# Chain products of an RWKV-7 layer issued in turn for the two column halves, and their output copy issued a step later

## The chip, the cores and the metric

The kernel runs on one core of a Trainium2 chip. The metric is the device time of one execution in microseconds, from the runs of the kernel before: 2830.11 us median of three (2828.12 to 2833.1). Times inside an execution come from one profiled execution.

## The reference

One layer takes x (2048 frames of 1024 channels), projects it, and feeds two token mixers: an S5 state space on 512 channels and an RWKV-7 recurrence of eight heads of width 64. Their outputs go through an output projection, a norm and a residual, then through a squared-ReLU feed-forward network. The part that the change touches is the recurrence:

```python
def step(S, inp):
    r_t, w_t, k_t, v_t, kk_t, a_t = inp
    sa = jnp.einsum('bhvk,bhk->bhv', S, -kk_t)
    S = (S * w_t[:, :, None, :]
         + sa[..., None] * (kk_t * a_t)[:, :, None, :]
         + v_t[..., None] * k_t[:, :, None, :])
    return S, jnp.einsum('bhvk,bhk->bhv', S, r_t)
```

The kernel computes it in chunks of 64 frames: inside a chunk with matrices (Gram products and a triangular inverse), from chunk to chunk with the state.

## The kernel before

The work has two stages. Stage one (`phase1`) handles four blocks of 512 frames; each block has four units of two heads, so 16 units. A unit is projected by dense 128x128 by 512 products (`preps`), gets Gram products and inverses, and then its chain of eight chunks runs (`chain`, line 1212). The 16 chains run one after another, 128 steps in all. The S5 mixer and part of the output projection run beside them. Stage two (`phase2`) has the gates, the output projection, the norms and the feed-forward products, which use a Strassen-Winograd scheme with sums of tiles on VectorE.

The order of all instructions is made by a planner in the kernel's own Python. Every kind of work is a generator; `merge` (line 447) always advances the one with the earliest due time by the planner's own clock, shifted by a constant for its kind (`OFFSETS`, line 249). `BURST` and `MARGIN` (line 247) pull forward the dense kinds (`DENSE`) of stage one when the planner thinks that TensorE has too little work in a stretch of time. `B1` and `B2` (line 245) weigh elementwise steps that read PSUM, for stage one and two. The planner prices a product in `price` (line 144); its flag `nc.pair` lowers the price of a single-precision product from 1.68 to 0.88 ns a column. It changes no instruction. The Gram products (line 1062) already set it. Every engine executes its instructions in the order in which they are emitted.

One step of a chain (loop from line 1222) works on one PSUM tile `cu` of two:
- two products of `wr` with `sv` into `uo` (partitions 0 to 63 and 64 to 127), and on GpSimd the decayed state `s0p`
- a copy of the upper half of `uo` to `rs`, on VectorE or ScalarE, whichever the planner has free
- two products of the inverse with `rs` into `us`, and a copy of it, negated, into `sv`
- two state products of `bet` with `sv` into `ss`: 128 rows, 64 columns, output in partitions 0 to 63
- two output products of `lat` (`lb` in the code) with `sv` into `uo[64:128]`: 64 rows, 64 columns, output in partitions 64 to 127
- the state sum `ss + s0p` on VectorE, the input of the next step, and on ScalarE the copy of `uo[64:128]` to the unit's output tile `ot`, and the signal `("ch", unit, step)`

Each of these products is single precision and appears in the trace as two records. The group norm (`gnorm`, line 1263) and the reuse of Gram buffers wait for the signals. Since one helper issues every instruction, all rows of the trace name line 108; tiles tell the work apart.

Of the kernel before, what the change touches and what calls it, by code (L numbers as in the profile page):

```python
# [241 lines left out]


D, NL, SR, TR, GR = 4, 2, 6, 14, 3
B1, B2 = 467, 4782
ORDER, ORDER0 = 'ugkrv', 'krugv'
SLACK, BURST, MARGIN = 199, 3048, 300
DENSE = ('preps', 'rwouts')
OFFSETS = {'s5_tables': -42, 's5_params': -395, 'norms': 352, 'inputs': -39, 'finals': 122, 'rwouts': -625, 'substitutes': -68, 'dense': -786, 'posts': -223, 'hns': 688, 's5_lane': 1208, 'chains': -22, 'zfirst': 262, 'inverses': 214, 's5_setup': 208, 'toks': 77, 'gramss': -173, 'x_loads': -2522, 'rwin': -59, 'f_loads': -91}


KEPT = ("w_in", "heads")
# [2 lines left out]
class K:  # L255
# [191 lines left out]
    def merge(self, streams):  # L447
# [6 lines left out]
        while any(x not in self.kept for x in h) or self.eq:  # L454
            r = [x for x in h if x[3] is None]
            b = BURST if nc.needy(MARGIN) else 0.0
            x = min(r, key=lambda x: (x[1] - (b if x[0].__name__ in DENSE else 0.0)
                                      + OFFSETS.get(x[0].__name__, 0.0), x[2])) if r else None
            e = self.elem()
# [752 lines left out]
    def chain(self, u):  # L1212
        nc, ep = self.nc, self.ep
        yield from self.need(("inv", u["s"]), ("bet", u["s"], 1), ("sv", u["s"]), "s5p")
        b, j, pc, wr, lb, bet, sv, yb = (u[n] for n in ("b", "j", "pc", "wr", "lb", "bet", "sv", "yb"))
        st = self.st[j // 2][64 * (j % 2):64 * (j % 2) + 64]
        nc.scalar.copy(sv[0][0:64, :, 0, :], st)
        if u["s"] >= 2:
            yield from self.need(("gno", u["s"] - 2))
        ot = u["ot"] = self.t(ep, [128, 4, 2, 64], "ot", bufs=2)  # L1220
        yield
        for c in range(8):
            q, i = divmod(c, 4)
            cu = self.t(self.pcu, [128, 384], "cu")
            uo = cu[:, 0:128].rearrange("p (h v) -> p h v", h=2)
            us = cu[0:64, 128:256].rearrange("p (h v) -> p h v", h=2)
            ss = cu[0:64, 256:384].rearrange("p (h v) -> p h v", h=2)
            for h in range(2):
                nc.tensor.matmul(uo[:, h, :], lhsT=wr[q][:, h, i, :], rhs=sv[q][:, h, i, :], start=h == 0, stop=False,
                                 skip_group_check=True)  # L1230
            s0 = self.t(self.sm, [64, 2, 64], "s0p", bufs=2)
            nc.gpsimd.tensor_tensor(out=s0, in0=sv[q][0:64, :, i, :], in1=pc[:, :, c:c + 1].to_broadcast([64, 2, 64]),
                                    op=ALU.mult)
            yield
            rs = self.t(self.sm, [64, 2, 64], "rs", bufs=2)
            if self.sooner(-27):
                nc.vector.tensor_copy(rs, uo[0:64])
            else:
                nc.scalar.copy(rs, uo[0:64])
            yield  # L1240
            for h in range(2):
                nc.tensor.matmul(us[:, h, :], lhsT=yb[:, 8 * h + c, :], rhs=rs[:, h, :], start=False, stop=True,
                                 skip_group_check=True)
            yield
            if self.sooner(-27):
                nc.vector.tensor_scalar(out=sv[q][0:64, :, i, :], in0=us, scalar1=-1.0, scalar2=None, op0=ALU.mult)
            else:
                nc.scalar.activation(out=sv[q][0:64, :, i, :], in_=us, func=AF.Copy, scale=-1.0)
            yield
            for h in range(2):  # L1250
                nc.tensor.matmul(ss[:, h, :], lhsT=bet[q][:, i, 64 * h:64 * h + 64], rhs=sv[q][:, h, i, :], start=False, stop=True,
                                 skip_group_check=True)
            for h in range(2):
                nc.tensor.matmul(uo[64:128, h, :], lhsT=lb[q][:, h, i, :], rhs=sv[q][0:64, h, i, :], start=False,
                                 stop=True, skip_group_check=True)
            yield
            nxt = sv[(c + 1) // 4][0:64, :, (c + 1) % 4, :] if c < 7 else st
            nc.vector.tensor_tensor(out=nxt, in0=ss, in1=s0, op=ALU.add)
            nc.scalar.copy(ot[64 * (c % 2):64 * (c % 2) + 64, c // 2], uo[64:128])
            self.fire(("ch", u["s"], c))  # L1260
            yield

    def gnorm(self, u):

# [1196 lines left out]
```

## Time and profile before

| what | value |
|---|---|
| median of three runs | 2830.11 us (2828.12 to 2833.1) |
| the profiled execution's own time | 2819.17 us |
| its span, first to last instruction | 2817.4 us |
| mean granted TensorE clock | 0.938 |
| TensorE busy | 2609.1 us, 93% |
| VectorE busy | 2218.6 us, 79% |
| ScalarE busy | 1298.0 us, 46% |
| GpSimd busy | 399.0 us, 14% |
| chains, first to last record | 172.5 to 1197.5 us |

Busy time counts an instruction from start to end; products overlap in TensorE's pipeline, so the distance between two starts is what a product costs the stream, and its duration is longer than that. The granted clock is 1.0 at 2.4 GHz and 0.5 at 1.2 GHz; a value between is a mean over a stretch.

### The profile page before, as it was taken

To read this page: it belongs to the slowest core of one execution; us is meant where nothing else is said; L and a number is where in the kernel's file an instruction comes from. 1 tells how busy PE (TensorE), PEld (TensorE's weight loads), DVE (VectorE), ACT (ScalarE), POOL (GpSimd) and SP (SyncE) were. 2 spreads that over 40 slices of the span, in tenths; PEclk is the share of its full clock that TensorE was granted. 3 is DMA by queue.
4 is the path that set the end of the run, shared out by engine and by line. 5 is a ranking of instruction groups with operands and counts; after the bars stand their busy time and mean duration, and the time that the engine had idled before them with its cause. 6 is when DMAs were issued, how large, how long until landed. Compare 5 with 4: busy or idle time off the path is not lost. (4 is left out here: it accounts for less than half of the span.)

```text
span 2817.4 us, 42634 instructions
## 1 busy us (share of the span) xinstructions
PE 2609.1 (93%) x14168; PEld 2039.9 (72%) x14168; DVE 2218.6 (79%) x4414; ACT 1298.0 (46%) x2783; POOL 399.0 (14%) x519
## 2 busy tenths in 40 slices
PE   6699999999999999989778899999999999999995
PEld 4466777677777777767647677678888888778884
DVE  6887777777777667579758888888777889988887
ACT  4454554454444344356245555666665222432221
POOL 0122222232222111211001000000000000021002
PEclk9788888999999998999879999999999999999997
DMA  6745564555656458876877877865669665666662
GB/s 207 236 147 174 156 186 136 172 169 156 193 173 197 141 160 263 266 185 210 279 250 262 279 283 265 285 211 209 223 218 338 227 226 198 240 239 238 237 208 90
DMA packets 404635, 600.82 MB, mean 213 GB/s; under 512 B 131008, under 2 KB 158144, under 8 KB 404416
## 3 DMA queue, kind: packets, MB, share of 16 engines
q1 hardware_dynamic: 404416, 598.11, 64.2%
q8 instruction: 112, 1.84, 0.3%
q14 instruction: 107, 0.88, 0.1%
HBM read 381.03 MB, written 208.54 MB: 209 GB/s over the span
## 5 line engine op out<-in xcount | busy, mean ns | idle before, releaser
L108 PE MATMUL mm<-ahi,whl 128*128 128x512 f32 x1864 | 744.3, 437 | 23.3 <-ACT ahi L108 17.0
L108 ACT ACTIVATE t<-t 128x512 fp32r<-128x512 f32 (+2 forms) x837 | 491.9, 625 | 512.3 <-DVE t L108 407.7
L108 DVE TENSOR_TENSOR t<-t 128x512 fp32r<-128x512 f32 (+2 forms) x829 | 562.3, 707 | 88.2 <-ACT t L108 84.0
L108 PE MATMUL mm<-t 128*128 128x512 f32 x2268 | 564.8, 401 | 28.3 <-DVE t L108 14.0
L108 PEld LDWEIGHTS mm<-t 128*128 128x128 f32 x2268 | 431.2, 192 | 143.9 <-ACT t L108 27.4
L108 PE MATMUL mm<-t,whl 128*128 128x512 f32 x1908 | 477.0, 405 | 19.9 <-DMA whl<-heads 9.5
L108 PEld LDWEIGHTS mm<-ahi,whl 128*128 128x128 f32 x1864 | 369.8, 199 | 120.7 <-ACT ahi L108 25.8
L108 PEld LDWEIGHTS mm<-t,whl 128*128 128x128 f32 x1908 | 364.5, 192 | 116.0 <-DMA whl<-heads 11.2
L108 DVE TENSOR_TENSOR t<-t,mm 128x512 f32<-128x512 f32 x592 | 401.7, 683 | 52.8 <-PE mm L108 41.4
L108 PE MATMUL mm<-alo,whl 128*128 128x512 f32 x932 | 386.7, 415 | 1.8 <-DVE alo L108 1.8
L108 PE MATMUL mm<-ahi,t 128*128 128x512 f32 x728 | 245.6, 399 | 2.8 <-DVE t L108 2.5
L108 PEld LDWEIGHTS mm<-alo,whl 128*128 128x128 f32 x932 | 186.1, 200 | 32.4 <-DVE alo L108 10.9
L108 POOL TENSOR_TENSOR t<-t 128x512 fp32r<-128x512 f32 (+1 forms) x55 | 80.6, 1472 | 653.8 <-ACT t L108 312.9
L108 PEld LDWEIGHTS mm<-ahi,t 128*128 128x128 f32 x728 | 138.1, 190 | 38.4 <-DVE t L108 4.7
L108 PE MATMUL mm<-alo,t 128*128 128x512 f32 x364 | 145.4, 399 | 0.0
L108 POOL TENSOR_TENSOR s0p<-sv,pc 64x128 f32<-64x128 f32 x128 | 73.7, 576 | 488.0 <-DVE sv L108 404.6
L108 DVE TENSOR_TENSOR whl<-raw,whl 128x512 fp32r<-128x512 f32 x128 | 92.0, 718 | 61.0 <-ACT whl L108 59.7
L108 ACT ACTIVATE whl<-t 128x512 fp32r<-128x512 f32 x120 | 72.8, 623 | 112.2 <-PE mm L108 64.9
L108 ACT COPY ot<-cu 64x128 f32<-64x128 f32 x128 | 33.6, 262 | 196.1 <-DVE sv L108 164.1
L108 ACT ACTIVATE whl<-raw 128x512 fp32r<-128x512 f32 x140 | 87.4, 625 | 75.1 <-DVE raw L108 26.6
L108 DVE TENSOR_TENSOR sub<-sub 64x15 f32<-64x15 f32 (+7 forms) x480 | 105.2, 219 | 10.3
L108 PE MATMUL gr<-con,t 128*128 128x2 f32 (+1 forms) x360 | 57.1, 283 | 56.9 <-DVE t L108 25.0
(351 smaller groups left out, 3415.7 us busy)
## 6 DMA issues: line engine op xcount, KB each, us to landing
fT<-t SPq DMA_DIRECT2D x384, 256.0 KB
t<-fT SPq DMA_DIRECT2D x235, 256.0 KB
whl<-w_in SPq DMA_DIRECT2D x108, 512.0 KB
alo<-fT SPq DMA_DIRECT2D x88, 256.0 KB
w_in<-whl SPq DMA_DIRECT2D x36, 512.0 KB
t<-hT SPq DMA_DIRECT2D x64, 256.0 KB
raw<-in_w_up_dram SPq DMA_DIRECT2D x64, 256.0 KB
t<-in_w_up_dram SPq DMA_DIRECT2D x64, 256.0 KB
```

What stands on the lines that cost most here:

```text
L108: getattr(self.eng, op)(*args, **kw)
```

## The change

Three things change. In the step of a chain the four last products are issued as state, output, state, output, with the planner's lower price. The copy to `ot` and its signal are issued in the next step, behind the copy to `rs` (for a unit's last step: at the end of the chain). And the planner's constants have other values: `B2`, `BURST`, `MARGIN` and seven of the offsets.

```diff
-B1, B2 = 467, 4782
+B1, B2 = 467, 5750
-SLACK, BURST, MARGIN = 199, 3048, 300
+SLACK, BURST, MARGIN = 199, 3120, 382
 OFFSETS: dense -786 to -769, posts -223 to 22, hns 688 to 1272,
          s5_lane 1208 to 1546, x_loads -2522 to -4141,
          rwin -59 to -118, s5in (none) to -165
@@ chain
+        def out(c, uo):
+            nc.scalar.copy(ot[64 * (c % 2):64 * (c % 2) + 64, c // 2], uo[64:128])
+            self.fire(("ch", u["s"], c))
+
         yield
         for c in range(8):
...
             yield
+            if c:
+                out(*owed)
             for h in range(2):
                 nc.tensor.matmul(us[:, h, :], lhsT=yb[:, 8 * h + c, :], rhs=rs[:, h, :], start=False, stop=True,
                                  skip_group_check=True)
...
             yield
+
+            nc.pair = True
             for h in range(2):
                 nc.tensor.matmul(ss[:, h, :], lhsT=bet[q][:, i, 64 * h:64 * h + 64], rhs=sv[q][:, h, i, :], start=False, stop=True,
                                  skip_group_check=True)
-            for h in range(2):
                 nc.tensor.matmul(uo[64:128, h, :], lhsT=lb[q][:, h, i, :], rhs=sv[q][0:64, h, i, :], start=False,
                                  stop=True, skip_group_check=True)
+            nc.pair = False
             yield
             nxt = sv[(c + 1) // 4][0:64, :, (c + 1) % 4, :] if c < 7 else st
             nc.vector.tensor_tensor(out=nxt, in0=ss, in1=s0, op=ALU.add)
-            nc.scalar.copy(ot[64 * (c % 2):64 * (c % 2) + 64, c // 2], uo[64:128])
-            self.fire(("ch", u["s"], c))
-            yield
+            owed = c, uo
+            yield
+        out(*owed)
+        yield
```

The offsets are written here as a list; in the code they are one dictionary.

## Rows read from the trace of the kernel before

**Rows 1.** The page, busy time of an engine: us, share of the span, instructions.
```profile
PE 2609.1 (93%) x14168; PEld 2039.9 (72%) x14168; DVE 2218.6 (79%) x4414; ACT 1298.0 (46%) x2783; POOL 399.0 (14%) x519
```
**Rows 2.** Stretches: busy us of each engine, granted clock, DMA share, GB/s.
```profile
172.00:1198.00 1026.00, 990.27 (x7268) 761.93 (x7269) 746.14 (x1924) 477.38 (x1287) 263.68 (x389) 0.92 0.60 180
1198.00:1620.00 422.00, 356.80 (x1433) 274.09 (x1432) 329.81 (x512) 210.54 (x370) 34.86 (x33) 0.90 0.75 244
1620.00:2400.00 780.00, 770.59 (x3277) 616.20 (x3276) 647.48 (x1029) 401.93 (x713) 20.65 (x15) 0.99 0.68 242
```
**Rows 3.** Waits of TensorE, 172 to 1198: us in total, times, longest.
```profile
PE cu L108 <- ACT sv L108: 8.8, 9, 2.3
PE cu L108 <- ACT rs L108: 8.3, 9, 3.4
PE mm L108 <- ACT ahi L108: 3.8, 4, 1.6
...
PE gr L108 <- ACT t L108: 1.3, 3, 0.8
...
PE mm L108 <- ACT t L108: 0.5, 1, 0.5
```
**Rows 4.** Timeline of TensorE in one step: start, us busy, what, records.
```profile
314.33 0.39 PE L108 MATMUL mm<-alo,whl 128*128 128x512 f32 x1
314.56 0.40 PE L108 MATMUL mm<-ahi,whl 128*128 128x512 f32 x1
314.88 0.44 PE L108 MATMUL cu<-rs,inv 64*64 64x64 f32 x4
...
316.15 0.45 PE L108 MATMUL cu<-sv,bet 128*64 128x64 f32 x4
316.52 0.44 PE L108 MATMUL cu<-sv,lat 64*64 64x64 f32 x4
316.89 0.50 PE L108 MATMUL mm<-ahi,whl 128*128 128x512 f32 x1
```
**Rows 5.** Timeline, narrow windows that end inside a group: records begun by then.
```profile
310.72 0.27 PE L108 MATMUL cu<-sv,bet 128*64 128x64 f32 x1
...
310.72 0.33 PE L108 MATMUL cu<-sv,bet 128*64 128x64 f32 x2
...
310.72 0.39 PE L108 MATMUL cu<-sv,bet 128*64 128x64 f32 x3
...
311.10 0.27 PE L108 MATMUL cu<-sv,lat 64*64 64x64 f32 x1
```
**Rows 6.** A state product's record (shortest, median, longest, ns); timeline of one state sum.
```profile
L108 PE MATMUL cu<-sv,bet x512: 222/222/371, 178.1 to 1196.9; 128*64 128x64 f32 x171
...
311.57 0.28 DVE L108 TENSOR_TENSOR sv<-cu,s0p 64x128 f32<-64x128 f32 x1 [0.84 <-PE cu L108]
```
**Rows 7.** Timeline, two places where products of one shape lie in different parts.
```profile
565.67 1.16 PE L108 MATMUL gr<-kr,be 64*128 64x128 f32 x16
566.76 0.50 PE L108 MATMUL mm<-ahi,whl 128*128 128x512 f32 x1
...
415.29 0.27 PE L108 MATMUL cu<-rs,inv 64*64 64x64 f32 x1
415.30 0.21 PE L108 MATMUL po<-yc,sub 64*48 64x16 f32 x1
```
**Rows 8.** Waits of ScalarE, 172 to 1198, and its timeline in one step.
```profile
ACT ot L108 <- DVE sv L108: 164.1, 99, 5.0
...
ACT ot L108 <- DVE st L108: 31.5, 16, 8.4
...
841.30 0.26 ACT L108 COPY rs<-cu 64x128 f32<-64x128 f32 x1 [0.71 <-PE cu L108]
842.49 0.27 ACT L108 ACTIVATE sv<-cu 64x128 f32<-64x128 f32 x1 [0.92 <-PE cu L108]
```
**Rows 9.** Waits of TensorE, 1198 to 1620: the longest of ten.
```profile
PE gr L108 <- DVE t L108: 20.5, 5, 8.6
```

More of the change, by code (lines that the diff above doesn't have):

```diff
@@ L244 @@
 D, NL, SR, TR, GR = 4, 2, 6, 14, 3
-B1, B2 = 467, 4782
+B1, B2 = 467, 5750
 ORDER, ORDER0 = 'ugkrv', 'krugv'
-SLACK, BURST, MARGIN = 199, 3048, 300
+SLACK, BURST, MARGIN = 199, 3120, 382
 DENSE = ('preps', 'rwouts')
-OFFSETS = {'s5_tables': -42, 's5_params': -395, 'norms': 352, 'inputs': -39, 'finals': 122, 'rwouts': -625, 'substitutes': -68, 'dense': -786, 'posts': -223, 'hns': 688, 's5_lane': 1208, 'chains': -22, 'zfirst': 262, 'inverses': 214, 's5_setup': 208, 'toks': 77, 'gramss': -173, 'x_loads': -2522, 'rwin': -59, 'f_loads': -91}
+OFFSETS = {'s5_tables': -42, 's5_params': -395, 'norms': 352, 'inputs': -39, 'finals': 122, 'rwouts': -625, 'substitutes': -68, 'dense': -769, 'posts': 22, 'hns': 1272, 's5_lane': 1546, 'chains': -22, 'zfirst': 262, 'inverses': 214, 's5_setup': 208, 'toks': 77, 'gramss': -173, 'x_loads': -4141, 'rwin': -118, 'f_loads': -91, 's5in': -165}
 KEPT = ("w_in", "heads")
```

## The prediction

> **What bounds the kernel now.** I read four views in this order: the table of stretches, the waits of TensorE, the timeline of one step of a chain, and the waits of ScalarE.
>
> The page gives TensorE as busy for 93% of the span [rows 1], but the chains of this change live in one stretch only, 172 to 1198 us, so the stretch is what counts. There TensorE is busy for 990 of 1026 us, VectorE for 746 and ScalarE for 477 [rows 2]. The busy time of pipelined products is modelled, so I checked it from the other side: the thirteen rows of TensorE's waits in this stretch add up to 36.7 us; five of them stand in [rows 3]. So in the first stage TensorE's instruction stream is the bound. The reader should see that a microsecond added to or taken from that stream is a microsecond of the span, less a few that existing waits swallow. The chain of 128 steps isn't the bound: a step starts about every 8 us on average (1026 / 128), and most of that time TensorE works on dense products between a step's parts.
>
> After 1198 us no chain runs. There TensorE waits for 64.9 us between 1198 and 1620 us (ten rows, the longest is in [rows 9]), and its granted clock over that stretch is 0.90 against 0.99 in the next [rows 2].
>
> **Part 1: the order of the four products.** One step ends with two state products (tile 128x64, output in partitions 0 to 63) and then two output products (tile 64x64, output in partitions 64 to 127). Each is two records of TensorE. The group is 0.74 us long: it begins at 316.15 and the next dense product starts at 316.89 [rows 4]. Inside the group, from an earlier step, taken in narrow windows: after one record the busy time is 0.27, after two 0.33, after three 0.39 [rows 5], and a record lasts 0.22 [rows 6]. So the second record starts 0.11 us after the first (0.33 - 0.22), the third 0.06 later, the fourth 0.06 later at 0.23; the first output record then starts 0.38 after the beginning (311.10 against 310.72), which is 0.15 behind the fourth. The output products repeat it: 0.37 from 316.52 to 316.89.
>
> So a record that follows one of the same shape costs 0.06, the second record after a change of shape 0.11, and a change of shape 0.15. The change of shape is where the question lies, because here the products before and after it already lie in different column halves, need nothing of each other, and still didn't run together. The same 0.09 (0.15 - 0.06) extra is seen where a 64x64 product follows a dense 128x128 one: 0.32 (314.56 to 314.88) where dense ones follow each other at 0.23 (314.33 to 314.56) [rows 4].
>
> Products of one shape in different parts of the array do run together. Sixteen records of the Gram products, shape 64x128 in the two row halves in turn, take 1.09 us [rows 7], 0.14 for a couple though each lasts 0.27. A 64x64 product of a chain and a 64x48 one of an inverse start 0.01 us apart (415.29 and 415.30) [rows 7]. So what decides is whether the shape stays the same, and the change makes it alternate: 128x64, 64x64, 128x64, 64x64. The Trainium skill, page "TensorEngine Tiling (Array Packing)", section "Key Properties", says that "Changing tiling mode (not just tile) drains the TensorE"; the rows agree, with 0.15 in place of 0.06.
>
> After the change the group has four couples of records, each 0.11 to its second record and 0.15 to the next shape: 4 x 0.26 = 1.04 us, against 0.74. That is +0.30 a step, and 128 steps give +38 us, all on the bound. The lower price counts only the two extra changes, 2 x (0.15 - 0.06) = 0.18, or +23 us. I take the upper one, because the slow second record stands behind both changes of shape in the rows. Waits that are not of the chain's own (16 of the 36.7 us) can swallow a little of it; I take 3 us. Result +35.
>
> The state sum on VectorE waits for the group's end as before: in the step of 310.72 it starts at 311.57 [rows 6], when the output products of 0.44 us from 311.10 are done, not the state products. The chain's own latency therefore grows by the same 0.30 us; that is counted once, since TensorE is what passes.
>
> **Part 2: the output copy one step later.** Today ScalarE stands idle in front of this copy until the state sum on VectorE is done: 164.1 and 31.5 us, 115 times [rows 8]. Everything behind it in ScalarE's queue waits too. After the change the copy stands behind the next step's copy of the right side, when its products and the sum are long done, so this idle time goes. What it is worth is what TensorE waits for ScalarE: 8.8, 8.3, 3.8, 1.3 and 0.5 us, 22.7 in all [rows 3]. The first two are for copies of the chain itself. These wait for products of their own step, which need the state sum as the output copy did and take longer than its 0.26 us, so they hardly change. The other three give 5.6; I take 5, between 0 and 22.7. The cost: 0.26 us of ScalarE between two copies of the chain. In the step of 841 us these stand at 841.30 and 842.49 [rows 8], and ScalarE was idle for 0.92 of the distance, so TensorE's products cover the copy. Without this cover it would cost 128 x 0.26 = 33 us. No DMA is issued by the moved step. Its signal, for which the reuse of Gram buffers two units on and the group norm wait, comes some 2 to 3 us later; a unit has eight steps of about 8 us, so only the last unit's norm shows it, for under 1 us.
>
> **Part 3: the altered constants.** They reorder two things: dense products of the first stage (burst, margin, S5 offset) and the loads, splits and sums after 1198 us (six offsets and the weight for evacuations). No row shows how a new order runs. Bounds: half of the 64.9 us of waits gone is -32; the first stretch at a granted clock of 0.90 instead of 0.92 is 2% of 1026, +20 us. I take the middle, -6.
>
> Sum: +35 - 5 - 6 = **+24 us**. The profiled execution has a span of 2817.4 and a time of 2819.2 us; it would become 2843. The median of the runs, 2830.1, lies 0.4% above it, and I carry the 24 us over to it: **2854 us**.
>
> **The rivals.** First, the column halves do work side by side (ends faster). Then each output record hides behind a state record: the group shrinks from 0.74 to about 0.37 to 0.41, saving some 0.35 x 128 = 45 us, and with the other parts -56: 2774. It decides if an output record starts within 0.06 us of the state record before it. For it stand the couples of [rows 7]; against it the 0.15 of [rows 5], where exactly these two products in exactly these halves didn't. The Trainium skill, page "TensorE: Matmul & The Clock Gate", section "Why this matters for your kernels", says that small-M products whose outputs lie in different column groups run at the same time; no run here shows that for tiles of two different sizes. Chance 0.07.
>
> Second, the new order gives back more than the products cost (faster). Place: TensorE's waits and its clock between 1198 and 1620 us. That stretch at 0.97 instead of 0.90 would be some 29 us shorter, with half of the waits 61. From 30 us on it cancels the rest of the sum, from 36 on the kernel is measurably faster; at 50 the time is 2830 + 35 - 5 - 50 = 2810. For it: the constants that move all act there. Against it: none is tied to one of the waits, which spread over ten releasers. Chance 0.12.
>
> Third, a draw within 0.2%, with the lower price of 23 us less 3, ScalarE freed for 10 and an order worth -12: 2828. Chance 0.12.
>
> Fourth, worse than forecast: the thinner stream lowers the granted clock in the first stretch to 0.90, +20 and nothing gained: 2880. It is part of slower.
>
> **How the numbers follow.** The forecast and the fourth rival hold 0.69 together. The likeliest is 2854. Downward the range takes the second rival's 2810, upward the fourth and a little more, 2886; outside are the first rival and the far ends of the order. A measurement of this kernel tells 0.2% (6 us) from no change: faster 0.19, same 0.12, slower 0.69.
>
> **What would show it.** In the changed trace the four couples of records should stand 0.26 us apart with the group at about 1.04 us; if it is under 0.5, the first rival holds. The rows of ScalarE's idle time before the output copy should be nearly gone. The stage of chains should end about 30 us later than 1198. The distance from there to the end should be near 1619 us; if it is 40 us less, the second rival holds. I am wrong if the chains' stage does not grow.

## The result, and the profile after

The changed kernel takes 2854.76 us (median of four runs, 2850.15 to 2858.67) against 2829.11 us, a ratio of 1.0091 with a 95% interval of 1.0066 to 1.0115. It is 26 us slower; 2854 was forecast.

The timeline of TensorE in one step of a chain comes first, from the changed kernel (start, us busy, what, records). It answers [rows 4].

```profile
613.03 0.40 PE L108 MATMUL mm<-ahi,whl 128*128 128x512 f32 x1
613.36 0.33 PE L108 MATMUL cu<-sv,bet 128*64 128x64 f32 x2
613.62 0.33 PE L108 MATMUL cu<-sv,lat 64*64 64x64 f32 x2
613.87 0.33 PE L108 MATMUL cu<-sv,bet 128*64 128x64 f32 x2
614.13 0.32 PE L108 MATMUL cu<-sv,lat 64*64 64x64 f32 x2
614.38 0.50 PE L108 MATMUL mm<-ahi,whl 128*128 128x512 f32 x1
```

The four couples stand 0.25 to 0.26 us apart, one strictly behind the other, and the group lasts 1.02 us (613.36 to 614.38) where it lasted 0.74 in [rows 4]. State and output products lie in different column halves and still don't run side by side.

The table of stretches, the chains' stage and the two that follow it (busy us of PE, PEld, DVE, ACT, POOL; granted clock, DMA share, GB/s):

```profile
172.00:1224.00 1052.00, 1030.58 (x7246) 785.55 (x7247) 746.16 (x1904) 480.00 (x1294) 261.31 (x385) 0.91 0.58 177
1224.00:1647.00 423.00, 355.23 (x1455) 272.26 (x1455) 322.44 (x506) 210.28 (x375) 40.63 (x37) 0.91 0.72 237
1647.00:2427.00 780.00, 765.70 (x3254) 613.15 (x3253) 652.17 (x1036) 403.38 (x715) 20.63 (x15) 0.98 0.69 245
```

Against [rows 2], TensorE is busy for 40 us more in the chains' stage, and the last record of a chain starts at 1224 instead of 1197. From there to TensorE's last record it is 1607 us, before it was 1601. So 27 of the 32 us by which this execution is longer than the profiled one before lie in the stage of the chains.

The waits of TensorE in the chains' stage (who for whom: us in total, times, longest), all nine rows:

```profile
PE cu L108 <- ACT sv L108: 6.3, 8, 1.7
PE gr L108 <- DVE lat L108: 6.1, 5, 2.1
PE cu L108 <- DVE rs L108: 2.8, 4, 1.2
PE mm L108 <- DVE alo L108: 2.1, 2, 1.3
PE gr L108 <- DVE cen L108: 1.5, 1, 1.5
PE cu L108 <- ACT rs L108: 1.2, 3, 0.4
PE mm L108 <- ACT ahi L108: 1.0, 1, 1.0
PE cu L108 <- DVE sv L108: 0.7, 2, 0.4
PE po L108 <- DVE inv L108: 0.5, 1, 0.5
```

They add up to 22.2 us; the thirteen rows to which those of [rows 3] belong add up to 36.7. Part of the difference is the new order: with it and the old turn of the products the waits are 32.6 us (a run below), so the longer groups swallowed some 10. The idle time of ScalarE in front of the output copy, from the same stretch, answers [rows 8]:

```profile
ACT ot L108 <- DVE sv L108: 21.3, 14, 2.8
...
ACT ot L108 <- DVE st L108: 14.8, 10, 3.3
```

It was 195.6 us in 115 waits and is 36.1 in 24. That large change in a row of waits bought no time that the runs below could measure.

### The profile page after: what moved, and what is told of

It reads as the page before. It is cut to its first block, busy times and chain, and to the rows that moved or that the text cites. A ratio compares the mean times of both kernels' runs of the same rounds, so it can differ in the third digit from the quotient of the medians.

```text
span 2849.7 us, 42658 instructions
## 1 busy us (share of the span) xinstructions
PE 2652.3 (93%) x14168; PEld 2066.8 (73%) x14168; DVE 2215.6 (78%) x4400; ACT 1301.4 (46%) x2796; POOL 401.5 (14%) x520
## 5 line engine op out<-in xcount | busy, mean ns | idle before, releaser
L108 PE MATMUL mm<-ahi,whl 128*128 128x512 f32 x1864 | 753.0, 440 | 28.0 <-ACT ahi L108 22.5
L108 ACT COPY t<-mm 128x512 f32<-128x512 f32 x120 | 69.7, 582 | 93.1 <-PE mm L108 72.5
L108 DVE TENSOR_TENSOR t<-raw,t 128x512 f32<-128x512 f32 (+1 forms) x136 | 95.3, 702 | 14.2 <-ACT t L108 10.7
```

The costliest lines, as they stand in the source:

```text
L108: getattr(self.eng, op)(*args, **kw)
```

## The experiments

The planner's order reacts to any altered price. So, where an edit was to be judged alone, the kernel issues the edited instructions in one order and books them in the planner in the other: every other instruction then keeps its place on its engine. In the code, `nc.nc` issues without booking and `nc.count` books without issuing. All kernels below were timed in five rounds; ratios, with their 95% intervals, are against the kernel before on the same chip, and what is called so many us faster or slower is worked out from the ratio.

### The alternation alone, and the change without it

On the kernel before, the four products are issued in turn and booked in the old order:

```diff
...
+            prods = [[(ss[:, h, :], bet[q][:, i, 64 * h:64 * h + 64], sv[q][:, h, i, :]) for h in range(2)],
+                     [(uo[64:128, h, :], lb[q][:, h, i, :], sv[q][0:64, h, i, :]) for h in range(2)]]
+            for x, h in [(0, 0), (1, 0), (0, 1), (1, 1)]:
+                o, w, y = prods[x][h]
+                nc.nc.tensor.matmul(o, lhsT=w, rhs=y, start=False, stop=True, skip_group_check=True)
+            for x, h in [(0, 0), (0, 1), (1, 0), (1, 1)]:
+                o, w, y = prods[x][h]
+                y = sv[q][0:64, h, i, :] if x else y
+                nc.count("tensor", "matmul", [o], [w, y], dict(lhsT=w, rhs=y))
...
```

These lines stand in place of the old ones of the four products.

> The kernel before with one edit: the four last products of a step are issued state, output, state, output. Every other instruction stands in the same place on its engine, and the constants are those of before. Theory (each change of shape drains the array): a group of four products lasts 1.03 us instead of 0.75, 128 times, so some +34 us, about 2863 us, ratio 1.010 to 1.013. Rival A (the order of everything else, which the new constants made, cost the time): ratio 0.998 to 1.003. Rival B (waits swallow most of the longer group): +10 us or less, ratio under 1.004.

Measured: 2860.06 us, ratio 1.0104 (1.0068 to 1.0139), so +29 us. The chains' stage ends at 1221 us, 24 later than before, and its row shows where: TensorE is busy for 1013 us against 990 in [rows 2].

```profile
172.00:1222.00 1050.00, 1013.31 (x7267) 771.68 (x7268) 746.98 (x1925) 478.42 (x1288) 261.72 (x389) 0.93 0.58 176
```

On the changed kernel the two lists are exchanged: issued state, state, output, output, booked in turn.

> The changed kernel with one edit: the four products are issued state, state, output, output again; every other instruction stands in the same place on its engine. Theory: it gives back 0.28 us a step, so 30 to 36 us, to about 2821 us, and ends at or a little below the kernel before, ratio 0.995 to 1.000 against it. Rival A: it stays at about 2853 us, ratio 1.008. If the rest of the change (late copy, new constants) were harmful, it would end above 1.002.

Measured: 2814.6 us, ratio 0.9965 (0.9936 to 0.9994). Between this and the changed kernel lie 1.26%, 36 us (give or take 11 by the two intervals), for the order of the four products alone. Rivals A and B fall. What is left of the change is 0.35% faster than before, 10 us, which the interval only just tells from nothing.

### The output copy, with everything else in place

On the kernel before, the copy of steps 0 to 6 is booked in its old place and issued behind the next step's copy to `rs` (the second piece stands earlier in the step):

```diff
-            nc.scalar.copy(ot[64 * (c % 2):64 * (c % 2) + 64, c // 2], uo[64:128])
+            owed = ot[64 * (c % 2):64 * (c % 2) + 64, c // 2], uo[64:128]
+            nc.count("scalar", "copy", [owed[0]], [owed[1]], {})
+            if c == 7:
+                nc.nc.scalar.copy(*owed)
```
```diff
                 nc.scalar.copy(rs, uo[0:64])
+            if c:
+                nc.nc.scalar.copy(*owed)
```

> The kernel before with one edit: the output copy of steps 0 to 6 of a unit is issued behind the next step's copy of the right side (the last step's stays). Every other instruction is in the same order. Theory: ScalarE's idle time before this copy, 204 us, nearly goes, but TensorE seldom waited for what stands behind it: 0 to 8 us faster, ratio 0.997 to 1.000. Rival C (ScalarE's idle time held up evacuations that TensorE needs): 15 to 22 us faster, ratio 0.992 to 0.995. Rival D (the copy between two copies of the chain delays it): slower by 10 us or more.

Measured: 2829.46 us, ratio 1.0004 (0.9976 to 1.0031): no difference, although the idle time in front of the copy fell as on the changed kernel. ScalarE's waits:

```profile
ACT ot L1264 <- DVE st L108: 27.4, 15, 5.3
ACT ot L1241 <- DVE sv L108: 22.2, 11, 4.4
```

TensorE's waits for ScalarE that are not the chain's own, 5.6 us in [rows 3], are still there, 5.9 us:

```profile
PE mm L108 <- ACT ahi L108: 3.4, 4, 1.5
...
PE gr L108 <- ACT t L108: 1.9, 5, 0.8
...
PE mm L108 <- ACT t L108: 0.6, 1, 0.6
```

So some 146 us less idle time on an engine that is busy for less than half of the stage bought nothing that the interval, from 7 us faster to 9 us slower, could show. The opposite was run on the changed kernel with the old order of products: booked late, issued in the old place.

```diff
         def out(c, uo):
-            nc.scalar.copy(ot[64 * (c % 2):64 * (c % 2) + 64, c // 2], uo[64:128])
+            nc.count("scalar", "copy", [ot[64 * (c % 2):64 * (c % 2) + 64, c // 2]], [uo[64:128]], {})
             self.fire(("ch", u["s"], c))
...
+            nc.nc.scalar.copy(ot[64 * (c % 2):64 * (c % 2) + 64, c // 2], uo[64:128])
             owed = c, uo
```

> The changed kernel with the old order of its four products and with the output copy issued in its old place, right behind the state sum; every other instruction stands where the changed kernel has it. Theory (what the late copy changes is the order that the planner makes with it in mind; its place in ScalarE's queue is worth nothing by itself, as on the kernel before): within 0.3% of the same kernel with the late copy, 2808 to 2823 us, ratio 0.994 to 0.999. Rival J (this order lives on the late copy's place): ScalarE is idle for some 200 us in front of it again and the time goes to 2850 us or more, ratio above 1.007.

Measured: 2817.43 us, ratio 0.9966 (0.9941 to 0.9992), the same as with the late copy (0.9965), although ScalarE is idle again for 193.7 us in front of the copy. Rivals C, D and J fall: the place of the copy in ScalarE's queue is worth less than some 10 us, the noise of these runs, on either order.

### The order that the constants and the price make

The changed constants alone on the kernel before (those of the diff):

> The kernel before with the changed constants alone; the order of all instructions is the planner's for these constants and the old products. Theory: between 12 us faster and 12 us slower, ratio 0.996 to 1.004. Rival A: it holds most of the measured slowdown, 15 us or more slower, ratio 1.005 to 1.009. Second rival of the prediction (the order gives back a lot): ratio under 0.988.

Measured: 2858.76 us, ratio 1.0108 (1.007 to 1.0145), +31 us. My theory's bounds were too narrow. Rival A's number for this kernel held, yet A fell as the cause of the measured slowdown: the changed kernel has these constants and loses its time to the turn of the products. The lower price alone:

```diff
+            nc.pair = True
             for h in range(2):
                 nc.tensor.matmul(ss[:, h, :], lhsT=bet[q][:, i, 64 * h:64 * h + 64], rhs=sv[q][:, h, i, :], start=False, stop=True,
                                  skip_group_check=True)
             for h in range(2):
                 nc.tensor.matmul(uo[64:128, h, :], lhsT=lb[q][:, h, i, :], rhs=sv[q][0:64, h, i, :], start=False,
                                  stop=True, skip_group_check=True)
+            nc.pair = False
```

> The kernel before with the planner's lower price for the four products alone: no instruction differs, only the order in which the planner emits the work; products in the old order, old constants. Theory (the order of the chains' stage is what the price and the constants move, to either side): between 12 us faster and 28 us slower, ratio 0.996 to 1.010; the difference lies before the last chain's end and shows in TensorE's waits and in the time at the half clock. Rival G (the price makes the order better by itself, and it is what made the changed kernel's order 10 us faster): ratio 0.995 to 0.998.

Measured: 2869.42 us, ratio 1.0155 (1.011 to 1.0201), +44 us, with not one instruction more or less. That is beyond my bound of 28 us too, and rival G falls. Both together:

> The kernel before with the changed constants and the lower price together; products in the old order, output copy in its old place. Theory (price and constants belong together: the constants are a set for the order that this price makes): near the changed kernel with the old order of its products, 5 to 20 us faster than before, ratio 0.993 to 0.998; TensorE's waits and the half clock's time in the chains' stage are back to those of before or under them. Rival H (the two add up, and the late copy is what made the order good): 40 to 75 us slower, ratio 1.014 to 1.027.

Measured: 2886.79 us, ratio 1.0204 (1.0169 to 1.0238), +58 us. My theory that price and constants belong together falls; rival H's number held. To see whether the place of the copy cured it, the slow order of that kernel was run with the copies issued late (the edit shown for the kernel before):

> The kernel before with the changed constants and the lower price, and the copies of steps 0 to 6 issued late in ScalarE's queue, with every other instruction in the order of that slow version. Theory: still 45 to 60 us slower than before, ratio 1.016 to 1.021, since the order is what is slow. Rival J: most of the 58 us comes back, ratio under 1.007.

Measured: 2888.69 us, ratio 1.0214 (1.0169 to 1.0259). The slow order stays slow. So of rival H only the planner's side is left: with the changed constants and the lower price, the order made with the late copy booked is good with the copy in either place, and the order made without it is bad with the copy in either place. The good order was also made with the products booked in turn, and the signal of a step comes later in it; no run separates these from the copy.

Where the bad order of both together loses is seen in its chains' stage, first the stretch, then the longest waits of TensorE there:

```profile
172.00:1231.00 1059.00, 1000.57 (x7178) 766.07 (x7179) 737.99 (x1902) 469.21 (x1269) 259.88 (x385) 0.89 0.57 171
```
```profile
PE cu L108 <- DVE sv L108: 13.4, 13, 4.4
PE cu L108 <- ACT rs L108: 8.6, 10, 3.6
PE cu L108 <- ACT sv L108: 7.6, 12, 1.7
```

Its granted clock is 0.89 where it was 0.92 in [rows 2], and TensorE's waits are 58.9 us in place of 36.7. In the changed kernel with the old order of products the stretch reads

```profile
172.00:1186.00 1014.00, 981.34 (x7249) 755.54 (x7249) 746.37 (x1903) 480.09 (x1291) 260.84 (x385) 0.93 0.60 183
```

with 32.6 us of waits. In the three slow orders the waits are longer (55 to 59 us) and the clock is lower (0.89 to 0.91) than before; what sets them off isn't shown. The order of both together loses 33 us in the chains' stage (last chain record at 1230 instead of 1197) and as much behind it (1640 us to TensorE's last record instead of 1601), the constants alone and the price alone nearly all in the chains' stage (1226 and 1242, with 1606 and 1605 behind). Each of these is a single execution: the order of both together, with its copies issued late, ended its chains at 1216 us, while its ratio was 1.02 as well. Which booking tips the planner into a bad order isn't settled.

### The same shape for both products

If the change of shape is what costs, output products over 128 rows should overlap with the state products. The lower half of their weights (`at`, last read by the inverse) is set to zero once the inverse is done, so the products are the same in value:

```diff
-            lb.append(lat[0:64])
+            lb.append(lat)
...
+        for q in range(2):
+            nc.nc.gpsimd.memset(at[q], 0.0)
         yield
         self.fire(("inv", s))
...
-                nc.tensor.matmul(uo[64:128, h, :], lhsT=lb[q][:, h, i, :], rhs=sv[q][0:64, h, i, :], start=False,
-                                 stop=True, skip_group_check=True)
+            prods = [[(ss[:, h, :], bet[q][:, i, 64 * h:64 * h + 64], sv[q][:, h, i, :]) for h in range(2)],
+                     [(uo[64:128, h, :], lb[q][:, h, i, :], sv[q][:, h, i, :]) for h in range(2)]]
...
```

The products are then issued from `prods` and booked as in the first diff of this part.

First on the kernel before, in turn, with the order of everything else kept:

> The kernel before with the four products alternating, and with output products of the same shape as the state products: they run over 128 rows, and the lower half of their weights is set to zero on GpSimd at the end of each inverse (32 memsets more, after the last use of what stood there). Everything else is in the same order, the constants are those of before. Theory (the shape decides, not the place): products in the two column halves now overlap as the Gram products do, a group takes 0.42 to 0.50 us in place of 0.75, so 30 to 40 us faster, ratio 0.986 to 0.991. Rival E (column halves never overlap for these products, only the drain goes): eight records follow each other at 0.06, a group takes 0.60, 15 to 20 us faster, ratio 0.993 to 0.996. Rival F (alternation itself costs, whatever the shape): 30 us slower.

Measured: 2809.05 us, ratio 0.9939 (0.9912 to 0.9967). A group takes 0.38 us, less than expected. It shrank by 0.365 us, 46 us over 128 steps, but the kernel gained 17 only: TensorE's waits in the chains' stage rose from 36.7 to 56.7 us, and the last record of a chain starts 26 us earlier, at 1171. The time lies outside my theory's range and in that of rival E, but E's group of 0.60 us did not come. Rivals E and F fall. The old order of the four products with the same shape:

> As the run before it (same shape by 128 rows with zeros), but the four products in the old order: state, state, output, output. Theory: only the meeting of the second state and the first output product can overlap; a group takes 0.50 to 0.60 us, 18 to 30 us faster than before, ratio 0.990 to 0.994, and slower than the alternating one. Rival E: the same time as the alternating one, about 0.60 us a group.

Measured: 2809.04 us, ratio 0.9948 (0.9919 to 0.9976), a group of 0.39 us. The timeline of TensorE in one step (the four state records are issued before the four output records):

```profile
580.63 0.27 PE L1256 MATMUL cu<-sv,bet 128*64 128x64 f32 x1
580.65 0.27 PE L1256 MATMUL cu<-sv,lat 128*64 128x64 f32 x1
580.74 0.22 PE L1256 MATMUL cu<-sv,bet 128*64 128x64 f32 x1
580.75 0.22 PE L1256 MATMUL cu<-sv,lat 128*64 128x64 f32 x1
580.80 0.22 PE L1256 MATMUL cu<-sv,bet 128*64 128x64 f32 x1
580.81 0.22 PE L1256 MATMUL cu<-sv,lat 128*64 128x64 f32 x1
580.86 0.22 PE L1256 MATMUL cu<-sv,bet 128*64 128x64 f32 x1
580.87 0.22 PE L1256 MATMUL cu<-sv,lat 128*64 128x64 f32 x1
581.02 0.50 PE L108 MATMUL mm<-ahi,whl 128*128 128x512 f32 x1
```

TensorE itself starts the output records 0.01 to 0.02 us behind the state records, although all of these stand ahead of them in the program. So what was said ahead of the prediction, that every engine executes its instructions in the order in which they are emitted, doesn't hold for these records. My theory's 0.50 to 0.60 us falls: for these products their order in the program doesn't matter, the shape does.

On the changed kernel, in turn, and then in the old order (what the first text calls the first run is the padded alternating kernel above):

> The changed kernel (alternating, late copy, its constants) with output products of the same shape as the state products, as in the first run of this call. Theory: a group goes from 1.03 to 0.42 to 0.50 us, 128 times, some 70 us less than the changed kernel: 2775 to 2790 us, ratio 0.980 to 0.986 against before. Rival E: 0.60 us a group, 55 us less, ratio 0.988 to 0.992.

> The changed kernel with output products of the state products' shape (128 rows, zeros in the lower half of their weights) and with the old order state, state, output, output. Theory, after the runs with padding: the engine overlaps them whatever the order, a group takes 0.38 to 0.39 us, the time is that of the padded alternating kernel, about 2780 us, ratio 0.982 to 0.988. Rival I (the alternation is worth something on the changed kernel's order): 10 us slower than the alternating one or more, ratio 0.989 or above.

Measured: 2779.73 us, ratio 0.9844 (0.9798 to 0.989), and 2779.74 us, ratio 0.9828 (0.9802 to 0.9854). These beat both kernels, by 44 to 49 us the one before and by 70 to 74 the changed one; against the changed kernel with the old order of its products the padding gains 34 to 39. Rival I falls. In the first one's timeline the couples start 0.01 us apart, and the group takes 0.39 us (572.44 to 572.83):

```profile
572.44 0.27 PE L1265 MATMUL cu<-sv,bet 128*64 128x64 f32 x1
572.45 0.27 PE L1265 MATMUL cu<-sv,lat 128*64 128x64 f32 x1
572.55 0.22 PE L1265 MATMUL cu<-sv,bet 128*64 128x64 f32 x1
572.56 0.22 PE L1265 MATMUL cu<-sv,lat 128*64 128x64 f32 x1
...
572.83 0.50 PE L108 MATMUL mm<-ahi,whl 128*128 128x512 f32 x1
```

## Why the prediction held, point by point

**The bound.** TensorE's stream in the stage of the chains was the bound: 0.28 us more in a group came out as 29 us (old order) and 36 us (changed order) of 36 that 128 groups make. What I said of a microsecond taken from the stream holds less well: the padding took 46 us from the stream on either order, and gained 17 on the old one and 34 to 39 on the changed one. TensorE's waits in the stage grew by 20 us on the one and by 12 on the other.

**Part 1, the products.** Forecast 1.04 us a group and +35 us, measured 1.02 us and +29 to +36. The terms read from [rows 4, 5] repeat in the changed trace: 0.11 to a second record, 0.15 to the next shape. The step that carried the forecast was to read the meeting of state and output products in the old trace as a trial of the change. The reason given, that the shape decides and not the place, is shown by the runs with padding: beside the same kernel without it, they alter nothing on TensorE but the rows of the output products, 64 to 128. That the number of columns must agree too is not shown; [rows 7] has 64x64 and 64x48 records side by side. The Trainium skill, page "TensorEngine Tiling (Array Packing)", section "Key Properties", says that a change of the tiling mode, and not of the tile alone, drains TensorE. The runs agree: a group with its shapes in turn took 1.02 us, with one shape and its places in turn 0.38, and 0.39 with its places one after the other. The waits swallowed nothing on the old order (36.7 and 36.8 us) and some 10 us on the changed one, where I had put down 3.

**Part 2, the copy.** Forecast -5 us, measured 0 on both orders, with a noise that doesn't exclude -5. The rows decide: the failing step was to count TensorE's waits for ScalarE that are not the chain's own (5.6 us in [rows 3]) as caused by what stood in front of them in the queue; I had no row for that, and they are 5.9 us with the idle time gone.

**Part 3, the constants.** Forecast -6 us, measured -10 for the order of the changed kernel. The value fits by luck. The sum had no term for what the lower price and the booked copy do to the order, and the price alone made it 44 us slower. The bounds of -32 and +20 were mis-sized: four orders that the planner made from pieces of the change lie at -10, +31, +44 and +58 us. I had bounded the loss by a clock of 0.90 in the first stretch; the worst order shows 0.89 and 22 us of waits more besides, and loses in the second stage too. I had also expected the constants to act mostly behind the chains. There the changed kernel is 6 us longer, and the gain lies in the chains' stage.

**The rivals.** The first (column halves side by side) did not happen, though its mechanism is real when the shapes agree. The second (an order that outweighs the products) did not reach its 36 us: the order gave 10, and in its place, between the chains' end and 1647 us, TensorE still waits for 67.6 us at a clock of 0.91. The third (a draw) is excluded by the interval of the ratio. Of the fourth there is a trace only: the clock of the chains' stage is 0.91, with the old turn of the products 0.93.

## What to carry to other kernels

Before products are packed into parts of the array, make their tile shapes equal, in rows too and if need be with zeros: a couple then cost one product here, while with 128x64 and 64x64 each further switch cost 0.14 us, a little more than the 0.12 of a product of 64 columns in a run of its own shape. Look in the old trace for a place where the two kinds already meet; it is the experiment. Where a planner makes the order, hold that order fixed to price an edit, since its reaction to a price or a constant was here worth as much as the edit and more (-10 to +58 us against 29 to 36). Idle time on an engine off the bound is no measure of a gain, and a shorter stream pays in full only as far as the work around it can follow.

## What was not expected of the hardware

Single-precision products of one shape in two column halves start 0.01 us apart, and they do so even when all products for one half are issued before those for the other, as the step at 580.63 shown above tells. It looks as if each half had a queue of its own; no run shows what lies behind it. Eight records took 0.38 to 0.39 us, the same as four records of one half alone (0.37 to 0.38 in [rows 4] and [rows 5]).
